# Winograd gate and up products of a decoder block: a sixth tile's first products beside the norms, down-weight sums in other tiles, one row tile transposed a turn sooner

## The chip, the core and the metric

One NeuronCore of a Trainium2 chip runs the whole kernel. TensorE (PE) multiplies, with its weight loads listed apart as PEld; VectorE (DVE), ScalarE (ACT) and GpSimd (POOL) do the elementwise work; SyncE (SP) issues the DMAs, which one queue takes in program order. The metric is the device time of one execution in microseconds (us); less is better.

## What is computed

One decoder layer in float32 on 1024 tokens of width 1024 with 16 meta tokens ahead of them. The part that the change touches is the end of the attention half and the SwiGLU half:

```python
h = h + rms_norm(mix @ w_out, ln_post_mix)
hn = rms_norm(h, ln_pre_ffn)
gu = hn @ w_gate_up                      # 1024 x 5632
ff = (silu(gu[..., :D_FF]) * gu[..., D_FF:]) @ w_down     # D_FF = 2816
h = h + rms_norm(ff, ln_post_ffn)
```

Each float32 product is made of three fp32r products: high by high, high by low and low by high part of operands that ACT (the rounded copy, a CAST) and DVE (the remainder, a subtraction) split.

## The kernel before

Gate and up are one Winograd scheme with seven half-size products in the place of eight. The hidden width is walked in `NF` = 22 tiles of 128 columns, `f_` = 0 to 21. A tile's seven products are of 12 matmuls each (four blocks of the inner dimension, three part products), and are numbered by `recipe`: 1 (`11` by `11`), 3 in the code of `first_products` or 2 in `recipe` (`12` by `21`), 5 (`s1` by `t1`), 6, 7, 3 and 4. The left operands `s1` to `s4` are sums of the weights that POOL makes (`combos`, tiles `cw`), the right operands `t1` to `t4` are sums of normed rows (`combine_rows`, tiles `c3`, `c1`, `c2`, `c4`), which PE then transposes.

**The norm stretch.** PE multiplies the last rows of the attention output (`half_out`, tiles `pz`), and beside that the row tiles `t` = 0 to 7 are normed in turns `n` = 0 to 9, written out by hand: ACT takes the sums of squares (`square_sum`, into `junk`; `ry` for the first norm, `rh` for the second), POOL the root, DVE `post_norm` and `second_norm`. `transposes` puts the two halves of a row tile through PE (tiles `tz` and `tzt`, from two PSUM banks, so that the third transposition waits until the remainder of the first is taken), ACT makes the high part (`b11h`, `b21h`, `bt3h` ...), DVE the low part (`b11l` ...). `unit()` emits the next piece of PE's other work in this stretch: 16 pieces of `half_out`, and then four pieces of six matmuls for each tile that is taken ahead: products 1 and 2 of tiles 3 and 4 (`SNAP`) and of 0, 1 and 2. The six PSUM banks hold those of tiles 0 to 2; those of 3 and 4 are copied to SBUF (`early`). `prepare_gate` loads a gate tile (`wgg`) and splits it into `a11` and `a12`, in the turns that `preps` names.

**The product stretch.** A loop over `f_` multiplies five products in tiles taken ahead (`ahead`) and seven in the others, all on PE in program order. Beside each product ACT and DVE split a block of the next tile, and POOL makes the sums of the next but one. Product 4 of an ahead tile is `held` until after the first product of the next. `store_acts` makes four sums of two finished tiles on POOL and stores them; `store_down` loads 256 rows of `w_down` (`rd`, one buffer of 1 MB), makes four sums on POOL and stores them (`down`). Both stand at the end of every second tile, from `f_` = 2 on. A last stretch multiplies the stored sums.

The engines keep the written order in both stretches; only SP's DMAs are ordered by the scheduler.

Of the kernel before, what the change touches and what calls it, by code (L numbers as in the profile page):

```python
# [21 lines left out]
P = 128  # L22
# [75 lines left out]
def hymba_kernel(ctx, tc, x, meta, rel_bias, g_pre_mix, g_post_mix, g_pre_ffn, g_post_ffn,  # L98
# [45 lines left out]
    dram = ctx.enter_context(tc.tile_pool(name="dram", bufs=1, space=DRAM))  # L144
# [1060 lines left out]
    def halves(t):  # L1205
        return y_of[t][:, 0:HALF], y_of[t][:, HALF:]

    def combine_rows(t):

        (b11, b21), (b12, b22) = halves(t - 4), halves(t)  # L1210
        t3, t1, t2, t4 = c = [bp.tile([P, HALF], F32, name=f"c{n}_{t}", tag="cb", bufs=6) for n in (3, 1, 2, 4)]
        rows_of[t] = dict(zip(("t3", "t1", "t2", "t4"), c))

        def first():
            pool.tensor_tensor(t3, b22, b12, op=ALU.subtract)
            pool.tensor_tensor(t1, b12, b11, op=ALU.subtract)

        return (first, lambda: pool.tensor_tensor(t2, t3, b11, op=ALU.add),
                lambda: dve.tensor_tensor(t4, b21, t2, op=ALU.subtract))

    rows_of = {}

# [8 lines left out]
        dve.tensor_tensor(lo, tp, f(hi), op=ALU.subtract)  # L1231


    op_homes = iter("gggg" + "wwww" + "gg" + "ggwww" + "oooow" + "ggggo" + "wwwwo" + "ggggo" + ("wwwwooo" + "ggggooo") * NF)
    o_n = [0]

    def op_tile(name):
# [69 lines left out]

    banks = {}

    N_AHEAD, SNAP = 5, (3, 4)  # L1310
    p1_of, early_of = {}, {}

    def first_products(f_):
        for i, (an, bn) in ((1, ("11", "11")), (3, ("12", "21"))):
            banks[f_, i] = b = bank(f"q{i}_{f_}")
            for part in range(2):
                product(b, f_, an, bn, True, i == 3, part)
                if part == 0:
                    yield None
            if f_ not in SNAP:  # L1320
                yield lambda: None
            elif i == 1:
                both = snp.tile([P, 2, HALF], F32, name=f"early{f_}")
                p1_of[f_], early_of[f_] = both[:, 0], both[:, 1]
                yield lambda f_=f_, b=b: act.copy(p1_of[f_], b)
            else:
                yield lambda f_=f_, b=b: dve.tensor_tensor(early_of[f_], b, p1_of[f_], op=ALU.add)

    def blocks():

# [20 lines left out]

    pinned.update(PINB)
    first_sum(2)
    preps = {0: 3, 1: 4, 4: 0, 5: 1, 6: 2}
    for n in range(4):
        gate = prepare_gate(preps[n], act) if n in preps else None
        if n:
            square_sum(n + 1, "rh", junk[0])
        unit(2)
        second_norm(n)  # L1360
        if n:
            transposes(halves(n - 1)[0], "11", n - 1)
        unit()
        if n:
            transposes(halves(n - 1)[1], "21", n - 1)
        unit()
        post_norm(n + 2)
        first_sum(n + 3)
        if gate:
            run(gate)  # L1370
    third = {}
    for n in range(4, 10):
        gate = prepare_gate(preps[n], act) if n in preps else None
        if n < 7:
            square_sum(n + 1, "rh", junk[0])
        if n == 6:
            b_op["t2"], b_op["t4"] = [[wap.tile([P, 4, HALF], F32R, name=f"bt{i}{x}", tag="wo", bufs=4) for x in "hl"]
                                      for i in (2, 4)]
            t1h, t1l, t3h = [h2p.tile([P, 4, HALF], F32R, name=f"b{x}", tag="late", bufs=3) for x in ("t1h", "t1l", "t3h")]
            b_op["t1"], b_op["t3"] = (t1h, t1l), (t3h, t3l)  # L1380
        if n >= 6:
            late = rows_of[n - 2]
            transposes(late["t3"], "t3", n - 2, third[n - 2])
        if n < NT:
            second_norm(n)
        if 5 <= n < 9:
            first, second, third[n - 1] = combine_rows(n - 1)
            first()
        if n == 4:
            transposes(halves(3)[0], "11", 3)  # L1390
        unit()
        if n >= 6:
            transposes(late["t1"], "t1", n - 2, (lambda: post_norm(n + 2)) if n + 2 < NT else lambda: None)
        elif n == 5:
            transposes(halves(4)[1], "22", 4, lambda: post_norm(7))
        else:
            post_norm(6)
        unit()
        if n == 4:
            transposes(halves(3)[1], "21", 3)  # L1400
        elif 6 <= n < 9:
            transposes(halves(n - 1)[1], "22", n - 1)
        first_sum(n + 3)
        if 5 <= n < 9:
            second()
        if n == 7:
            early = iter((raw_tile("cw00", (P, 2, 4, P)), bp.tile([P, 2, 4, P], F32, name="cw01", tag="gfb", bufs=1)))
            pending = combos(0, lambda name: next(early))
            pending[0]()
        elif n == 8:  # L1410
            pending[1]()
        unit()
        if n >= 6:
            transposes(late["t2"], "t2", n - 2)
        if n >= 7:
            unit()
        if n >= 6:
            transposes(late["t4"], "t4", n - 2)
        if gate:
            run(gate)  # L1420
    unit(20)
# [12 lines left out]
    def s_tile(f_, c):  # L1434
        s_of[f_, c] = fp.tile([P, HALF], F32, name=f"s{f_}{c}", tag="s", bufs=6)
        return s_of[f_, c]
# [63 lines left out]
        s4 = combined(f"s4_{i}", "S", ALU.subtract, a12, s2)  # L1500
        sp.dma_start(act_dram["4"][i], s4)

    def store_down(i):

        r = fp.tile([P, 2, 2, HALF], F32, name=f"rd{i}", tag="rd", bufs=1)
        sp.dma_start(r, w_down[0, 2 * i * P:2 * (i + 1) * P, :].rearrange("(j p) (h c) -> p j h c", p=P, h=2))
        (b11, b12), (b21, b22) = [[r[:, j, h] for h in range(2)] for j in range(2)]
        pool.tensor_tensor(b22, b22, b12, op=ALU.subtract)
        pool.tensor_tensor(b12, b12, b11, op=ALU.subtract)
        pool.tensor_tensor(b11, b22, b11, op=ALU.add)  # L1510
        pool.tensor_tensor(b21, b21, b11, op=ALU.subtract)
        for n, x in (("1", b12), ("2", b11), ("3", b22), ("4", b21)):
            sp.dma_start(down_dram[n][i], x)
# [29 lines left out]
            parts_of[n].append(hl)  # L1543

    held = None
    pending = combos(1, cw_tile)
    for f_ in range(NF):
        ahead = f_ < N_AHEAD
        order = (5, 6, 3, 7, 4) if ahead else (1, 5, 6, 2, 7, 3, 4)
        names = ("s1", "s2", "s4", "s3", "22") if f_ + 1 < N_AHEAD else ("11", "s1", "s2", "12", "s3", "s4", "22")  # L1550
        parts = [lambda: [load(n) for n in range(3)]] + [lambda: None] + [lambda n=n: split_step(n) for n in range(3)]
        if f_ + 1 < NF:
            first, second = pending
            parts = [lambda n=n: split_block(f_ + 1, n) for n in names]
            if len(order) < len(names):
                s2, s3 = parts[1:3], parts[3:5]
                parts = [parts[0], lambda: [c() for c in s2], lambda: [c() for c in s3]] + parts[5:]
            s0, s1 = parts[0:2]
            parts[0] = lambda: (first(), s0())
            parts[1] = lambda: (second(), s1())  # L1560
        parts = iter(parts)
        for i, n in enumerate(order):
            if n == 4 and ahead:
                held = f_
                next(parts, lambda: None)()
                continue
            if i == 0 and ahead:
                if f_ in SNAP:
                    s_of[f_, 0] = early_of[f_]
                    act.activation(early_of[f_], early_of[f_], AF.Silu)  # L1570
                else:
                    after(f_, 1)
                    after(f_, 2)
            multiply(f_, n, next(parts, lambda: None))
            if i == 0 and held is not None and held != f_:
                multiply(held, 4)
                held = None
        if f_ + 2 < NF:
            pending = combos(f_ + 2, cw_tile)
        j = f_ - 1  # L1580
        if j > 0 and j % 2:
            store_acts(j // 2)
            store_down(j // 2)
    store_down(NP - 1)
    store_acts(NP - 1)
    pinned.difference_update(("pe", "act", "dve", "pool"))
    op_st.close()
# [134 lines left out]
```

## Time and profile before

| | us |
|---|---|
| median of three runs | 1218.53 |
| lowest and highest | 1215.46, 1219.6 |
| the profiled execution | 1218.1 |
| its span, first to last instruction | 1216.1 |
| PE busy in the span | 1162.9 |
| DVE, ACT, POOL busy | 786.1, 551.4, 502.6 |

The span is what the trace covers; 2.0 us of the execution lie around it. Busy times are sums per engine. PE is busy in 96% of the span, so time can come only from stretches where it waits, where its clock is low, or from matmuls that leave a stretch in which it is full.

### The profile page before, as it was taken

Reading aid. Unit: us, or ns where it says so; the run is one execution under the profiler, and the core shown is the slowest. Engines: PE = TensorE matmul, PEld = TensorE weight load, DVE = VectorE, ACT = ScalarE, POOL = GpSimd, SP = SyncE. Lnnn points to the kernel's source line nnn. Section 1 sums busy time; section 2 is a strip of 40 time slices with the busy share of each in tenths; the row PEclk is TensorE's granted clock in tenths of the full one; section 3 lists DMA queues with packets and bytes.
Section 4 is the critical chain, followed back from the end, with each engine's and each line's share of the span. In section 5 each row is a group of like instructions: output and inputs, shape, how many; then the busy total and the mean of one; then the engine's idle time right before and its main releaser. Section 6 shows DMA issues by size and latency. Waiting matters only on the chain.

```text
span 1216.1 us, 17389 instructions
## 1 busy us (share of the span) xinstructions
PE 1162.9 (96%) x5967; PEld 987.1 (81%) x5967; DVE 786.1 (65%) x1637; ACT 551.4 (45%) x1174; POOL 502.6 (41%) x523
## 2 busy tenths in 40 slices
PE   7989999999999989987899999999999999999997
PEld 6978879998998777865787788888888887888886
DVE  6477876666666777888567755556555545556764
ACT  5366565555555451454442333333333325555531
POOL 7242334344333342326468665765566640000001
PEclk9999999999999999998999999999999999999999
DMA  7431223132121420363245545534455377676645
GB/s 231 133 97 30 57 66 101 45 80 59 41 69 41 148 87 26 97 241 104 79 138 189 175 164 185 175 134 157 147 183 173 129 252 260 224 236 214 225 151 196
DMA packets 135463, 168.36 MB, mean 138 GB/s; under 512 B 10644, under 2 KB 84372, under 8 KB 135374
## 3 DMA queue, kind: packets, MB, share of 16 engines
q1 hardware_dynamic: 135374, 167.25, 42.7%
q8 instruction: 47, 0.77, 0.3%
q14 instruction: 42, 0.34, 0.1%
HBM read 115.22 MB, written 46.56 MB: 133 GB/s over the span
## 4 chain that ended last, share of the span: by engine, by line
PE 43%; DVE 3%; POOL 3%; issue 2%; DMA 1%; ACT 1%; POOLq 0%; DVEq 0%; SPq 0%; ACTq 0%
PE q L113 26%; PE px L113 9%; PE py L113 7%; POOL rd L113 1%; POOL s L113 1%; DVE a L113 1%; DVE y L113 1%; DVE s L113 1%; POOL cw L113 0%; DMA rd<-in_w_down_dram 0%; PE tzt L113 0%; DVE as L113 0%; DMA act<-s 0%; DMA wgu<-in_w_gate_up_dram 0%; DMA rab<-in_w_down_dram 0%
## 5 line engine op out<-in xcount | busy, mean ns | idle before, releaser
L113 DVE TENSOR_TENSOR hl<-rab,hl 128x512 fp32r<-128x512 f32 x154 | 102.2, 712 | 76.8 <-ACT hl L113 76.5
L113 DVE TENSOR_TENSOR as<-cw,as 128x512 fp32r<-128x512 f32 x78 | 79.9, 1028 | 69.1 <-ACT as L113 68.1
L113 PE MATMUL px<-hl,hl 128*128 128x512 f32 x528 | 122.5, 393 | 1.7 <-ACT hl L113 1.5
L113 ACT CAST hl<-rab 128x512 fp32r<-128x512 f32 x154 | 88.1, 619 | 78.9 <-PE py L113 27.1
L113 PEld LDWEIGHTS px<-hl,hl 128*128 128x128 f32 x528 | 100.2, 190 | 23.4 <-ACT hl L113 1.9
L113 PE MATMUL py<-hl,hl 128*128 128x512 f32 x396 | 90.2, 389 | 0.0
L113 PEld LDWEIGHTS py<-hl,hl 128*128 128x128 f32 x396 | 74.3, 188 | 15.4
L113 ACT ACTIVATE s<-s 128x512 f32<-128x512 f32 x42 | 26.6, 632 | 111.5 <-DVE s L113 111.4
L113 POOL TENSOR_SCALAR PF<-PF,lf 128x144 f32<-128x144 f32 (+3 forms) x64 | 51.3, 801 | 62.4 <-DVE lf L113 46.0
L113 POOL TENSOR_TENSOR cw<-wgu 128x512 f32<-128x512 f32 x22 | 29.6, 1346 | 114.8 <-DMA wgu<-in_w_gate_up_dram 106.3
L113 POOL TENSOR_SCALAR rf0v<-sa 128x1 f32<-128x1 f32 x1 | 0.6, 563 | 177.2 <-DVE sa L113 177.2
L113 POOL TENSOR_TENSOR s<-s,s 128x512 f32<-128x512 f32 x41 | 60.7, 1493 | 30.0 <-DVE s L113 25.2
L113 POOL TENSOR_TENSOR rd<-rd 128x512 f32<-128x512 f32 x44 | 66.4, 1508 | 10.4 <-DMA rd<-in_w_down_dram 7.8
L113 ACT ACTIVATE PF<-PF,nf 128x144 f32<-128x144 f32 (+3 forms) x64 | 50.6, 790 | 39.2 <-DVE nf L113 37.7
L113 DVE TENSOR_TENSOR a<-wgg,a 128x512 fp32r<-128x512 f32 x44 | 48.1, 1101 | 30.1 <-ACT a L113 30.1
L113 PE MATMUL q<-b11h,a 128*128 128x512 f32 x176 | 60.8, 404 | 4.5 <-ACT b11h L113 4.5
L113 ACT CAST as<-cw 128x512 fp32r<-128x512 f32 x78 | 47.6, 619 | 33.9 <-POOL cw L113 22.6
L113 POOL TENSOR_SCALAR P<-P,ls 128x272 f32<-128x272 f32 (+1 forms) x64 | 29.5, 479 | 77.2 <-DVE ls L113 66.3
L113 DVE TENSOR_TENSOR s<-q,s 128x512 f32<-128x512 f32 x62 | 42.6, 687 | 27.3 <-PE q L113 26.3
L113 PE MATMUL q<-b21h,a 128*128 128x512 f32 x176 | 59.1, 394 | 0.7 <-ACT b21h L113 0.7
L113 ACT COPY s<-q 128x512 f32<-128x512 f32 x40 | 23.5, 587 | 79.7 <-PE q L113 57.5
L113 PE MATMUL q<-bt1h,as 128*128 128x512 f32 x176 | 58.0, 391 | 1.4 <-ACT as L113 1.2
(491 smaller groups left out, 3408.1 us busy)
## 6 DMA issues: line engine op xcount, KB each, us to landing
rab<-act SPq DMA_DIRECT2D x77, 256.0 KB, 3.1
act<-s SPq DMA_DIRECT2D x75, 256.0 KB, 2.7
wgg<-in_w_gate_up_dram SPq DMA_DIRECT2D x27, 512.0 KB, 4.2
wgu<-in_w_gate_up_dram SPq DMA_DIRECT2D x22, 512.0 KB, 3.6
rd<-in_w_down_dram SPq DMA_DIRECT2D x11, 1024.0 KB, 6.9
down<-rd SPq DMA_DIRECT2D x44, 256.0 KB, 2.0
rab<-down SPq DMA_DIRECT2D x44, 256.0 KB, 3.3
wi<-in_w_in_dram SPq DMA_DIRECT2D x18, 512.0 KB, 3.7
```

Source lines behind the costliest of these rows:

```text
L113: i = fn(*a, **k)
```

## The change

It has three parts. First, `N_AHEAD` is 6 and `SNAP` has a third tile: tile 5's products 1 and 2 are made in the norm stretch, after those of 3 and 4. `prepare_gate` is called once more (tile 5 in turn 4, tiles 0, 1 and 2 one turn later each), and there are four more calls of `unit()`. The copies of tile 5 go to DRAM (`keep`, two stores) and come back at the start of `f_` = 4 (`bring_back`, two loads). Room for them is had by making `t2` and `t4` in place, in the row tiles themselves: `combine_rows` takes two new tiles of four buffers and not four of six. Second, row tile 3 is transposed at the end of turn 3, not within turn 4. Third, `store_down` is parted: `load_down` issues the load at the start of a tile and the sums stand at its end, in odd tiles from 5 on and in 12 and 18. The table of buffers (`op_homes`) is written anew to fit.

```diff
-        t3, t1, t2, t4 = c = [bp.tile([P, HALF], F32, name=f"c{n}_{t}", tag="cb", bufs=6) for n in (3, 1, 2, 4)]
-        rows_of[t] = dict(zip(("t3", "t1", "t2", "t4"), c))
+        t3, t1 = [bp.tile([P, HALF], F32, name=f"c{n}_{t}", tag="cb", bufs=4) for n in (3, 1)]
+        rows_of[t] = {"t3": t3, "t1": t1, "t2": b11, "t4": b21}
...
-        return (first, lambda: pool.tensor_tensor(t2, t3, b11, op=ALU.add),
-                lambda: dve.tensor_tensor(t4, b21, t2, op=ALU.subtract))
+        return (first, lambda: pool.tensor_tensor(b11, t3, b11, op=ALU.add),
+                lambda: dve.tensor_tensor(b21, b21, b11, op=ALU.subtract))
...
-    N_AHEAD, SNAP = 5, (3, 4)
+    N_AHEAD, SNAP = 6, (3, 4, 5)
     p1_of, early_of = {}, {}
+
+    snap_dram = dram.tile([P, 2, HALF], F32, name="snap_dram")
+
+    def keep(f_, b):
+        dve.tensor_tensor(early_of[f_], b, p1_of[f_], op=ALU.add)
+        if f_ == 5:
+            for i, x in enumerate((p1_of[f_], early_of[f_])):
+                sp.dma_start(snap_dram[:, i], x)
+
+    def bring_back(f_):
+        early_of[f_] = s_tile(f_, 0)
+        p1_of[f_] = fp.tile([P, HALF], F32, name=f"p1_{f_}", tag="s", bufs=6)
+        for i, x in enumerate((p1_of[f_], early_of[f_])):
+            sp.dma_start(x, snap_dram[:, i])
...
-    preps = {0: 3, 1: 4, 4: 0, 5: 1, 6: 2}
+    preps = {0: 3, 1: 4, 4: 5, 5: 0, 6: 1, 7: 2}
...
+        if n == 3:
+            transposes(halves(3)[0], "11", 3)
+            transposes(halves(3)[1], "21", 3)
         post_norm(n + 2)
...
-        if n == 4:
-            transposes(halves(3)[0], "11", 3)
         unit()
...
-        if n == 4:
-            transposes(halves(3)[1], "21", 3)
-        elif 6 <= n < 9:
+        if 6 <= n < 9:
...
-        if n >= 7:
+        if n >= 6:
             unit()
-        if n >= 6:
             transposes(late["t4"], "t4", n - 2)
+        if 7 <= n < 9:
+            unit()
...
+        if f_ == 4:
+            bring_back(5)
+
+        rd = load_down(n_down) if f_ >= 5 and (f_ % 2 or f_ in (12, 18)) else None
...
         if j > 0 and j % 2:
             store_acts(j // 2)
-            store_down(j // 2)
-    store_down(NP - 1)
+        if rd is not None:
+            store_down(n_down, rd)
+            n_down += 1
```

What stands where is shown at three places. The first is ACT at turns 3 and 4 (`b11h` from `tz112` is row tile 2, from `tz113` row tile 3; `sry6` and `srh5` are sums of squares of row tiles 6 and 5). Before:

```order
L113 CAST b11h_6542<-tz112_6765 128x4x128
L113 CAST b21h_6544<-tz212_6780 128x4x128
L113 ACTIVATE junk_6376,sry6_6796<-y6_5343 128x1024
L113 ACTIVATE junk_6376,srh5_6804<-y5_5342 128x1024
L113 CAST b11h_6542<-tz113_6811 128x4x128
L113 CAST b21h_6544<-tz213_6836 128x4x128
L113 ACTIVATE junk_6376,sry7_6843<-y7_5344 128x1024
L113 COPY early3_6835<-q1_3_6818 128x512
```

and now:

```order
L113 CAST b11h_6542<-tz112_6766 128x4x128
L113 CAST b21h_6544<-tz212_6781 128x4x128
L113 CAST b11h_6542<-tz113_6794 128x4x128
L113 CAST b21h_6544<-tz213_6801 128x4x128
L113 ACTIVATE junk_6376,sry6_6811<-y6_5343 128x1024
L113 ACTIVATE junk_6376,srh5_6819<-y5_5342 128x1024
L113 ACTIVATE junk_6376,sry7_6844<-y7_5344 128x1024
L113 COPY early3_6843<-q1_3_6826 128x512
```

Both casts of row tile 3 moved ahead of the squares of row tiles 6, 5 and 7.

The second is PE in turns 6 and 7 (`tzt24` is `t2` of row tile 4, `tzt44` its `t4`, `tzt35` `t3` of row tile 5; `q1_5` is product 1 of tile 5; the rows of matmuls up to the next transposition are one unit of six). Before:

```order
L113 MATMUL tzt24_6983<-ident_70,c2_4_6874 128x128 x4
L113 MATMUL tzt44_6990<-ident_70,c4_4_6875 128x128 x4
L113 MATMUL tzt35_7003<-ident_70,c3_5_6940 128x128 x4
L113 MATMUL q1_0_6975<-b11h_6542,a11_0_6857 128x512
L113 MATMUL q1_0_6975<-b11l_6543,a11_0_6857 128x512
L113 MATMUL q1_0_6975<-b11h_6542,a11_0_6857 128x512 x2
L113 MATMUL q1_0_6975<-b11l_6543,a11_0_6857 128x512
L113 MATMUL q1_0_6975<-b11h_6542,a11_0_6857 128x512
L113 MATMUL tzt15_7024<-ident_70,c1_5_6941 128x128 x4
```

and now:

```order
L113 MATMUL tzt24_6980<-ident_70,y0_5337 128x128 x4
L113 MATMUL q1_5_6972<-b11h_6542,a11_5_6858 128x512
L113 MATMUL q1_5_6972<-b11l_6543,a11_5_6858 128x512
L113 MATMUL q1_5_6972<-b11h_6542,a11_5_6858 128x512 x2
L113 MATMUL q1_5_6972<-b11l_6543,a11_5_6858 128x512
L113 MATMUL q1_5_6972<-b11h_6542,a11_5_6858 128x512
L113 MATMUL tzt44_6994<-ident_70,y0_5337 128x128 x4
L113 MATMUL tzt35_7009<-ident_70,c3_5_6939 128x128 x4
L113 MATMUL q3_5_7022<-b21h_6544,a12_5_6861 128x512
```

A unit stands between the transpositions of `t2` and `t4` where there was none, and the units here are tile 5's in the place of tile 0's.

The third is POOL at tiles 2 to 5 of the product stretch (`s1_0` to `s4_0` are the sums of `store_acts` for tiles 0 and 1, `rd0` the first down sums, `cw40` and `cw41` the weight sums of tile 4). Before:

```order
L113 TENSOR_TENSOR s1_0_7514<-s01_7265,s11_7363 128x512
L113 TENSOR_TENSOR s2_0_7517<-s1_0_7514,s00_7229 128x512
L113 TENSOR_TENSOR s01_7265<-s00_7229,s01_7265 128x512
L113 TENSOR_TENSOR s4_0_7522<-s10_7313,s2_0_7517 128x512
L113 TENSOR_TENSOR rd0_7525<-rd0_7525 128x512 x4
L113 TENSOR_TENSOR cw40_7509<-wgu4_7507 128x512
L113 TENSOR_TENSOR cw40_7509<-cw40_7509,wgg4_7505 128x512
L113 TENSOR_TENSOR cw41_7510<-wgg4_7505,wgu4_7507 128x512
L113 TENSOR_TENSOR cw41_7510<-wgg4_7505,cw40_7509 128x512
```

and now:

```order
L113 TENSOR_TENSOR s4_0_7554<-s10_7345,s2_0_7549 128x512
L113 TENSOR_TENSOR cw40_7541<-wgu4_7539 128x512
L113 TENSOR_TENSOR cw40_7541<-cw40_7541,wgg4_7537 128x512
L113 TENSOR_TENSOR cw41_7542<-wgg4_7537,wgu4_7539 128x512
L113 TENSOR_TENSOR cw41_7542<-wgg4_7537,cw40_7541 128x512
L113 TENSOR_TENSOR cw50_7652<-wgu5_7650 128x512
L113 TENSOR_TENSOR cw50_7652<-cw50_7652,wgg5_7648 128x512
L113 TENSOR_TENSOR cw51_7653<-wgg5_7648,wgu5_7650 128x512
L113 TENSOR_TENSOR cw51_7653<-wgg5_7648,cw50_7652 128x512
L113 TENSOR_TENSOR s1_1_7758<-s21_7494,s31_7605 128x512
```

The four down sums that stood ahead of tile 4's weight sums are gone from here; the first now stand behind those of tile 6. SP's rows at the end of that tile show what is queued behind the second load of down weights (`wgu7` is the up tile for `f_` = 7). Now:

```order
L113 DMA down1_0_156<-rd0_7769 128x512
L113 DMA down2_0_167<-rd0_7769 128x512
L113 DMA down3_0_178<-rd0_7769 128x512
L113 DMA down4_0_189<-rd0_7769 128x512
L113 DMA act11_2_81<-early4_6908 128x512
L113 DMA rd1_8042<-in_w_down_dram 128x2x1024
L113 DMA wgu7_7871<-in_w_gate_up_dram 128x8x128
L113 DMA wgg8_8022<-in_w_gate_up_dram 128x8x128
```

`rd1` is issued behind the four stores of `rd0`, whose buffer it takes, and `wgu7` behind `rd1`; before, at the same tile's load, `wgu7` stood behind `rd2` and one store of activations.

## Rows read from the trace of the kernel before

**Rows 1.** Stretches by window: length, busy time (count) per engine, PEclk, DMA share, GB/s.

```profile
540.00:550.00 10.00, 3.86 (x20) 2.59 (x18) 9.93 (x11) 4.19 (x8) 2.85 (x4) 0.78 0.16 66
550.00:560.00 10.00, 8.45 (x25) 6.08 (x26) 5.09 (x8) 3.90 (x10) 1.47 (x4) 0.71 0.23 94
...
750.00:800.00 50.00, 50.00 (x222) 41.42 (x221) 27.08 (x31) 17.94 (x32) 28.40 (x19) 1.00 0.48 155
```

**Rows 2.** Timeline of PE, norm stretch: start, length, what, count [idle before, releaser].

```profile
545.26 0.84 PE L113 MATMUL tz<-ident,y 128*128 128x128 f32 x4 [2.24 <-DVE b11l L113]
550.64 0.80 PE L113 MATMUL q<-b11h,a 128*128 128x512 f32 x1 [4.54 <-ACT b11h L113]
...
565.49 0.66 PE L113 MATMUL tzt<-ident,c 128*128 128x128 f32 x4 [1.42 <-POOL c L113]
```

**Rows 3.** Timeline of ACT at turns 4 and 5.

```profile
548.97 1.06 ACT L113 ACTIVATE junk<-y 128x1024 f32<-128x1024 f32 x1 [2.95 <-DVE y L113]
...
556.69 0.59 ACT L113 CAST b21h<-tz 128x512 fp32r<-128x512 f32 x1 [6.10 <-PE tz L113]
...
559.73 1.07 ACT L113 ACTIVATE junk<-y 128x1024 f32<-128x1024 f32 x1
```

**Rows 4.** Timeline of DVE at turns 3 to 5.

```profile
545.72 0.68 DVE L113 TENSOR_TENSOR b21l<-tz,b21h 128x512 fp32r<-128x512 f32 x1
...
550.62 0.69 DVE L113 TENSOR_TENSOR b11l<-tz,b11h 128x512 fp32r<-128x512 f32 x1 [0.57 <-ACT b11h L113]
...
557.31 0.69 DVE L113 TENSOR_TENSOR b21l<-tz,b21h 128x512 fp32r<-128x512 f32 x1 [2.95 <-ACT b21h L113]
559.35 1.30 DVE L113 TENSOR_TENSOR a<-wgg,a 128x512 fp32r<-128x512 f32 x2 [1.35 <-ACT a L113]
```

**Rows 5.** Waits of PE from 530 to 970 us: in total, times, longest.

```profile
PE tz L113 <- DVE bt3l L113: 2.3, 2, 1.5
...
PE tzt L113 <- DVE bt1l L113: 1.0, 2, 0.8
PE tzt L113 <- DVE bt2l L113: 1.0, 1, 1.0
```

**Rows 6.** Timeline of PE, first matmul of the product stretch.

```profile
600.07 0.53 PE L113 MATMUL q<-bt1h,as 128*128 128x512 f32 x1 [1.24 <-ACT as L113]
```

**Rows 7.** Timeline of PE, tiles 3 to 5 of the product stretch.

```profile
651.11 0.47 PE L113 MATMUL q<-bt3h,as 128*128 128x512 f32 x1 [1.28 <-DVE s L113]
...
667.53 0.39 PE L113 MATMUL q<-b11h,a 128*128 128x512 f32 x1
...
671.61 0.50 PE L113 MATMUL q<-bt4h,a 128*128 128x512 f32 x1 [1.20 <-DVE p L113]
```

**Rows 8.** Timeline of POOL, the same tiles.

```profile
638.99 6.50 POOL L113 TENSOR_TENSOR rd<-rd 128x512 f32<-128x512 f32 x4
645.45 1.29 POOL L113 TENSOR_TENSOR cw<-wgu 128x512 f32<-128x512 f32 x1
...
668.67 6.81 POOL L113 TENSOR_TENSOR rd<-rd 128x512 f32<-128x512 f32 x4
678.38 1.29 POOL L113 TENSOR_TENSOR cw<-wgu 128x512 f32<-128x512 f32 x1 [2.90 <-DMA wgu<-in_w_gate_up_dram]
```

**Rows 9.** Timeline of DVE, the same tiles.

```profile
669.17 1.78 DVE L113 TENSOR_TENSOR mix<-cw,mix 128x512 fp32r<-128x512 f32 x1
670.88 0.68 DVE L113 TENSOR_TENSOR p<-q,p 128x512 f32<-128x512 f32 x1
...
688.01 0.68 DVE L113 TENSOR_TENSOR mix<-cw,mix 128x512 fp32r<-128x512 f32 x1
```

**Rows 10.** DMA issues on the page: count, KB each, us to landing.

```profile
wgu<-in_w_gate_up_dram SPq DMA_DIRECT2D x22, 512.0 KB, 3.6
rd<-in_w_down_dram SPq DMA_DIRECT2D x11, 1024.0 KB, 6.9
down<-rd SPq DMA_DIRECT2D x44, 256.0 KB, 2.0
```

More of the change, by code (lines that the diff above doesn't have):

```diff
@@ L1231, in transposes @@
         dve.tensor_tensor(lo, tp, f(hi), op=ALU.subtract)
-    op_homes = iter("gggg" + "wwww" + "gg" + "ggwww" + "oooow" + "ggggo" + "wwwwo" + "ggggo" + ("wwwwooo" + "ggggooo") * NF)
+    op_homes = iter("gggg" + "wwww" + "gggg" + "wwwwg" + "oooog" + "wwwwo" + "ggggo" + "wwwwo" + "ggggo" + ("wwwwooo" + "ggggooo") * NF)
     o_n = [0]
@@ L1322, in first_products @@
             elif i == 1:
-                both = snp.tile([P, 2, HALF], F32, name=f"early{f_}")
+                both = (snp if f_ < 5 else bp).tile([P, 2, HALF], F32, name=f"early{f_}")
                 p1_of[f_], early_of[f_] = both[:, 0], both[:, 1]
@@ L1326, in first_products @@
             else:
-                yield lambda f_=f_, b=b: dve.tensor_tensor(early_of[f_], b, p1_of[f_], op=ALU.add)
+                yield lambda f_=f_, b=b: keep(f_, b)
     def blocks():
@@ L1501, in store_acts, with load_down, store_down @@
         sp.dma_start(act_dram["4"][i], s4)
-    def store_down(i):
+    def load_down(i):
         r = fp.tile([P, 2, 2, HALF], F32, name=f"rd{i}", tag="rd", bufs=1)
         sp.dma_start(r, w_down[0, 2 * i * P:2 * (i + 1) * P, :].rearrange("(j p) (h c) -> p j h c", p=P, h=2))
+        return r
+    def store_down(i, r):
         (b11, b12), (b21, b22) = [[r[:, j, h] for h in range(2)] for j in range(2)]
@@ L1545, in hymba_kernel @@
     held = None
+    n_down = 0
     pending = combos(1, cw_tile)
@@ L1582, in hymba_kernel @@
             store_acts(j // 2)
-            store_down(j // 2)
-    store_down(NP - 1)
+        if rd is not None:
+            store_down(n_down, rd)
+            n_down += 1
+    assert n_down == NP
     store_acts(NP - 1)
```

## The prediction, written before the changed kernel ran

> **What bounds the kernel now.** I read the windows by stage first. In the product stretch PE is full: 222 matmuls fill 50.00 of 50 us at the full clock, 0.225 us each, and DVE, ACT and POOL have idle time [rows 1]. A matmul that leaves this stretch is worth its whole 0.225 us. In the norm stretch it is otherwise: from 540 to 550 us DVE is busy for 9.93 of 10 us and PE for 3.86, and PE's granted clock is 0.78 there and 0.71 in the next 10 us, which is the 1.2 GHz level for part of both [rows 1]. So this stretch is bound by the chain from row tile to row tile, and PE has room. The timeline of PE names its two large waits: 2.24 us for `b11l`, and 4.54 us for `b11h` of row tile 3 [rows 2]. The timelines of ACT and DVE tell why. The cast of `b11h` stood behind the square of row tile 5, which waited 2.95 us for DVE's `post_norm`; the cast of `b21h` came 6.10 us later, since its transposition stands behind the first unit of products on PE; and the square of row tile 6, behind it, starts only at 559.73 [rows 3]. DVE meanwhile lost 0.57, 2.95 and 1.35 us [rows 4], 4.87 in all, though it was the engine that bounds.
>
> **Part 1, row tile 3 a turn sooner.** Nothing is added; eight transposing matmuls, two casts and two remainders change places. The first transposition can go no sooner than 545.26, since it still waits for the bank that row tile 2's `b11l` gives back [rows 2]. The second follows when `b21l` of row tile 2 ends, 545.72 + 0.68 = 546.40 [rows 4]. Each then goes through ACT (0.59 us a cast [rows 3]) and DVE. I count 0.3 us of DVE idle for each of the two, 0.6 in all, for the 4.87 that vanish, since `post_norm` of row tile 5, 6 and 7 and `second_norm` now follow one another without a cast between. DVE is thus 4.3 us ahead at the remainder of `b22`. ACT's square of row tile 6 no longer stands behind the late `b21h`; it now waits for `post_norm` of row tile 6 and starts about 4.3 us sooner, and with it the root on POOL and POOL's first `t3`, for which PE waited until 565.49 [rows 2]. That becomes 561.2. What is late next is still POOL's `t3`, at the same place. PE's first products of tile 3 can start at about 547.4, at the low clock, but they end before 561.2 at either level, so their speed costs nothing.
>
> **Part 2, tile 5 taken ahead.** Out of the product stretch go products 1 and 2 of tile 5: 24 matmuls x 0.225 = 5.4 us [rows 1]. The same 5.4 us enter the norm stretch after 561.2. Before, from 565.49 to the first product of tile 0 at 600.07 it was 34.6 us [rows 2, 6]. In these lie waits of 2.3, 1.0 and 1.0 us for `bt3l`, `bt1l` and `bt2l` [rows 5], 4.3 together, and at the end 1.24 us for the first weight split [rows 6], which stays. How much of 5.4 do the waits take up? The unit between `t2` and `t4` in turn 6 covers the 1.0 for `bt2l` and part of one for `bt1l`; those for `bt3l` stay in the main, since `bt3l` stands on DVE behind the two gate splits of each turn. The other three units stand in turns 7 and 8, where part of the waits remains. On the other side POOL now halts in turn 7: the first weight sums of tile 0 go into a raw buffer that the gate tile of turn 7 holds until DVE has split it. This stops no one before turn 9, and without POOL beside it DVE is faster: a remainder with both inputs in SBUF took 1.78 us while POOL worked and 0.68 alone, and a sum that reads PSUM took 0.68 even beside POOL [rows 8, 9]. I take 1.3 us as hidden. So the products start at 561.2 + 34.6 + 5.4 - 1.3 = 599.9, 0.2 us sooner than before. The bounds: with all of 5.4 hidden it is 4.3 sooner, the shift of part 1 alone (the waits sum to just 4.3, so this is a floor); with none hidden 561.2 + 34.6 + 5.4 = 601.2, 1.1 later.
>
> The Trainium skill ("GPSIMD Engine Reference", Key points) states that GpSimd shares its SBUF interfaces with VectorE and contends with its instructions of two SBUF inputs. The rows agree, with 1.78 against 0.68. If the page's rule were applied to every remainder of turns 7 and 8 as gained time, the start would come near the floor of the range above.
>
> What else comes with tile 5: one more copy on ACT, one more sum on DVE, and two casts and two remainders that leave tile 4's share of the product stretch for turn 7, where DVE and ACT have gaps. The four transfers of 256 KB (two stores, two loads) stand on SP behind nothing that waits long, and the loads have a whole tile's time; I cost them at nothing. If a load were late, PE would wait at the start of `f_` = 5; the load of twice that size takes 3.6 us [rows 10]. Reading tile 5's copies gives DVE a few more sums of 0.68 us, as tiles 3 and 4 have now. The in-place `t2` and `t4` are as many instructions as before.
>
> **Part 3, down sums elsewhere.** At `f_` = 2 POOL made four down sums, 6.50 us from 638.99, and the weight sums of tile 4 started only behind them, at 645.45 [rows 8]; ACT and DVE got their splits late, and PE waited 1.28 us at 651.11 [rows 7]. Now no down sum stands there, so tile 4's weight sums start 6.5 us sooner and this wait goes. At the end of `f_` = 4 PE waited 1.20 us for DVE's `p`, at 671.61 [rows 7], which stood behind a remainder of 1.78 us beside the down sums of 668.67 [rows 8, 9]. The down sums of the new first place come at the end of `f_` = 5, which is now the last tile taken ahead and the one with seven blocks to split in five products, so the same crowding moves there; but POOL starts them as soon as tile 6's weight sums are done, since the load is long there, and may be through when `p` comes. The trace can't decide between 0 and 1.2; I take half, 0.6. Beyond that PE shows no wait until the down stretch, so the load's 6.9 us [rows 10] that POOL no longer waits for are worth nothing there.
>
> **The sum**, against the profiled execution of 1218.1: 5.4 out of the product stretch, 0.2 by its earlier start, 1.28 and 0.6 of waits, 7.5 us in all: 1210.6. The median of the runs lies 0.4 above the profiled one, so 1211.0. By the bounds it is best 5.4 + 4.3 + 1.28 + 1.2 = 12.2 us, 1206.3, and at worst 5.4 - 1.1 = 4.3 us, 1214.2, if the waits of part 3 only move.
>
> **Rivals.** *Low clock again.* In the norm stretch the clock fell while PE waited and came back in the dense matmuls behind [rows 1, 2]. Now PE is done with tile 3 and the first half of tile 4 some 2 or 3 us before 561.2 and waits again. If the clock falls there, some 5 us of matmuls run at half speed, 2.5 us, of which little is hidden: 1213.5. Against it: the wait is about as long as the 2.24 that stands first in [rows 2], and part of it falls right behind 24 dense matmuls. The Trainium skill ("TensorE: Matmul & The Clock Gate", Part 1) has the array fall to its lower level when it idles; the trace agrees, and by that rule this rival is the one to expect if the wait grows.
>
> *The stretch grows, the waits move.* DVE or the banks bind in turns 6 to 8 with nothing hidden, tile 5 as a copied tile costs DVE at `f_` = 5 what tile 4 did, and both waits of part 3 come back one tile on, with 1 to 2 us for the extra sums of DVE. For it speaks how crowded DVE was there, with 1.78 us for one remainder right before `p` [rows 9]. It is 5.4 - 1.1 - 2 = 2.3 us: 1216.2, no change that can be told.
>
> *Slower: the up tile behind the down load.* `rd1` waits on SP until the stores of `rd0` have landed, and `wgu` of the tile after next stands behind it. If it comes late, POOL's weight sums are late, ACT is held at their cast with the copies behind it that free PSUM, and PE waits in product 7; the same in each of eight tiles with such a load. The price is what POOL starts later than some 10 us into the tile: at `f_` = 5 it started at 678.38, 10.85 after 667.53 [rows 7, 8], with no wait of PE from it, in a tile longer than the common one. By the rows, four weight sums of 1.29 us or more and four down sums of 6.5 to 6.8 [rows 8] end some 13 us into a tile, the stores take 2.0, then `rd` 6.9 and `wgu` 3.6 one after the other [rows 10], so `wgu` is there 6.5 us into the next tile of 84 x 0.225 = 18.9 us, 3 us before it decides. If the loads slowed each other by 5 us more, it would be 1.5 us in eight tiles: 1211 + 12 = 1223.
>
> That the change does nothing is out: PE's order shows tile 5's units in the norm stretch.
>
> **How the numbers follow.** The forecast has 0.60, the low clock 0.13, the grown stretch 0.19, the late up tile 0.08. The range leaves out the last and the outer edges of the others: 1206.5 to 1216.5. About 0.3%, 3.7 us, is what a measurement of this kernel can tell from no change, so faster means under 1214.9: the forecast, the low clock but for a little, and 0.05 of the grown stretch, 0.76 in all; the rest of the latter two is no change, 0.17; slower 0.07.
>
> **What would show it.** In the profile after: ACT's casts of `b11h` and `b21h` one behind the other at about 546 and 547; the first `tzt` at about 561; the first product of tile 0 near 600, so that the whole gain of 7 lies behind it; no wait of PE in `f_` = 3, and one of 0 to 1.2 us at the end of `f_` = 5. A first `tzt` at 565 would break part 1; a product stretch that starts after 602, part 2; a wait of PE in each odd tile from 7 on would be the slower rival.

## The result, and where the time went

The changed kernel takes 1237.78 us (median of four runs, 1235.58 to 1241.5) against 1216.99 before: 1.0167 times, 95% interval 1.0134 to 1.0199. That is slower by 20.8 us where 7.5 less was forecast.

The three stages tell where. The norm stretch is counted from the transposition that waits 2.2 us for `b11l` of row tile 2 to the first product of tile 0, the product stretch from there to the end of PE's last product (the first `px` less its wait), the down stretch from there to the end:

| us, from one trace each | norm stretch | product stretch | down stretch |
|---|---|---|---|
| before [rows 2, 6] | 54.81 | 395.62 | 220.4 |
| after | 55.04 | 420.57 | 219.6 |

The stages add up to 24.4 us more. In this trace the norm stretch also began 4.5 us sooner than before, at 540.76 where it was 545.26, so that the whole span is 19.9 us longer; the last section comes back to that.

The norm stretch came out close to what the prediction had. The timeline of PE after; the rows answer to [rows 2, 6]:

```profile
540.76 0.66 PE L113 MATMUL tz<-ident,y 128*128 128x128 f32 x4 [2.23 <-DVE b11l L113]
...
557.15 1.12 PE L113 MATMUL tzt<-ident,c 128*128 128x128 f32 x4 [4.47 <-POOL c L113]
...
595.80 0.50 PE L113 MATMUL q<-bt1h,as 128*128 128x512 f32 x1 [1.19 <-ACT as L113]
```

ACT casts row tile 3 in one go now, where [rows 3] had 6.10 us and the square between:

```profile
541.45 0.58 ACT L113 CAST b11h<-tz 128x512 fp32r<-128x512 f32 x1 [0.99 <-PE tz L113]
543.11 0.59 ACT L113 CAST b21h<-tz 128x512 fp32r<-128x512 f32 x1 [1.07 <-PE tz L113]
```

From 540.76 the first `tzt` is 16.39 us away, before it was 20.23; the first product is 55.04 us away, before 54.81. The loss lies behind it, in the product stretch. Its windows (columns as in [rows 1]):

```profile
700.00:800.00 100.00, 96.53 (x422) 78.69 (x421) 53.39 (x60) 33.32 (x59) 61.48 (x40) 1.00 0.42 141
800.00:900.00 100.00, 90.59 (x377) 73.36 (x376) 48.95 (x51) 30.66 (x55) 58.48 (x39) 0.95 0.51 171
900.00:1000.00 100.00, 92.03 (x385) 74.20 (x386) 55.70 (x58) 30.17 (x54) 67.65 (x45) 0.97 0.46 157
```

Where [rows 1] had 222 matmuls in 50 us, 444 in 100, there are now 422, 377 and 385, and the granted clock is under 1.00 in two of three windows. The waits of PE from 600 to 1000 us (in total, times, longest):

```profile
PE q L113 <- ACT s L113: 17.9, 9, 3.0
PE q L113 <- DVE p L113: 3.5, 5, 0.7
```

That is 21.4 us. One of these waits, in tile 8, is followed back here through four engines. PE comes first (the first row is the start of tile 8), then ACT:

```profile
717.20 0.39 PE L113 MATMUL q<-b11h,a 128*128 128x512 f32 x1
...
729.13 0.50 PE L113 MATMUL q<-bt3h,as 128*128 128x512 f32 x1 [0.89 <-ACT s L113]
```

```profile
726.60 0.62 ACT L113 CAST as<-cw 128x512 fp32r<-128x512 f32 x1 [5.54 <-POOL cw L113]
...
727.97 0.62 ACT L113 CAST as<-cw 128x512 fp32r<-128x512 f32 x1 [0.27 <-POOL cw L113]
728.50 0.58 ACT L113 COPY s<-q 128x512 f32<-128x512 f32 x1
```

Product 7 adds to what product 6 left in its PSUM bank, and the copy `s<-q` must have read that bank before. That copy stands on ACT behind the casts of tile 9's `s1` and `s2`, and ACT was held 5.54 us for them. POOL, with the time that it waited before each:

```profile
708.11 6.57 POOL L113 TENSOR_TENSOR rd<-rd 128x512 f32<-128x512 f32 x4
725.27 1.29 POOL L113 TENSOR_TENSOR cw<-wgu 128x512 f32<-128x512 f32 x1 [10.59 <-DMA wgu<-in_w_gate_up_dram]
...
731.28 6.48 POOL L113 TENSOR_TENSOR s<-s,s 128x512 f32<-128x512 f32 x4
742.36 1.29 POOL L113 TENSOR_TENSOR cw<-wgu 128x512 f32<-128x512 f32 x1 [4.60 <-DMA wgu<-in_w_gate_up_dram]
...
765.78 1.29 POOL L113 TENSOR_TENSOR cw<-wgu 128x512 f32<-128x512 f32 x1 [10.82 <-DMA wgu<-in_w_gate_up_dram]
```

And SP's queue (start and length of the issues):

```profile
709.87 5.16 SPq L113 DMA_DIRECT2D down<-rd  x4
...
715.60 1.86 SPq L113 DMA_DIRECT2D act<-s  x1
718.62 0.38 SPq L113 DMA_DIRECT2D rd<-in_w_down_dram  x1
719.09 0.42 SPq L113 DMA_DIRECT2D wgu<-in_w_gate_up_dram  x1
...
720.19 17.92 SPq L113 DMA_DIRECT2D act<-s  x6
738.20 0.39 SPq L113 DMA_DIRECT2D wgu<-in_w_gate_up_dram  x1
```

POOL, SP and the transfers close a loop. POOL ends the down sums at 708.11 + 6.57 = 714.68. SP, which stood at their stores, issues the last of them and must then wait until they have landed before `rd` may go into the same buffer (718.62); from 700 to 780 us the profile puts two waits of SP, 1.9 us, down to `down<-rd`. Only then comes `wgu` (719.09). At 725.27, 6.18 us after that issue and 10.59 us after its last work, POOL can go on. The other up tile stands behind six stores of the activations' sums, the last of which waits for POOL too: 4.60 us more. Before, in tiles of the same kind, POOL waited for `wgu` like this:

```profile
862.74 1.29 POOL L113 TENSOR_TENSOR cw<-wgu 128x512 f32<-128x512 f32 x1 [4.59 <-DMA wgu<-in_w_gate_up_dram]
...
876.58 1.29 POOL L113 TENSOR_TENSOR cw<-wgu 128x512 f32<-128x512 f32 x1 [7.46 <-DMA wgu<-in_w_gate_up_dram]
```

That is 12.05 us in a pair of tiles, and the next pair began at 900.80, 38.06 us behind the first: POOL kept PE's pace. In the changed kernel two tiles cost POOL 765.78 - 725.27 = 40.5 us, of which 4.60 + 10.82 = 15.4 are waits for its own tail. PE needs 2 x 84 x 0.225 = 37.8 us for two tiles. So POOL falls back 2.7 us in each pair of tiles; once the lead that it had is used up, PE waits about that long.

### The profile page after: what moved, and what is told of

The parts are those of the page before. It is cut to its first block, busy times and chain, and to the rows that moved or that the text cites. A ratio compares the mean times of both kernels' runs of the same rounds, so it can differ in the third digit from the quotient of the medians.

```text
span 1236.0 us, 17396 instructions
## 1 busy us (share of the span) xinstructions
PE 1166.4 (94%) x5967; PEld 985.4 (80%) x5967; DVE 786.4 (64%) x1640; ACT 550.7 (45%) x1172; POOL 508.7 (41%) x523
## 4 chain that ended last, share of the span: by engine, by line
PE 55%; POOL 14%; DMA 11%; DVE 9%; issue 8%; ACT 3%; SPq 0%; POOLq 0%; DVEq 0%; ACTq 0%
PE q L113 11%; PE px L113 9%; PE py L113 7%; DMA wgu<-in_w_gate_up_dram 6%; POOL cw L113 5%; POOL rd L113 3%; PE pvb L113 3%; POOL s L113 3%; PE pqb L113 3%; PE of L113 3%; PE pqa L113 2%; PE pk L113 2%; PE sf L113 2%; PE tf L113 2%; PE pya L113 1%
## 5 line engine op out<-in xcount | busy, mean ns | idle before, releaser
L113 DVE TENSOR_TENSOR as<-cw,as 128x512 fp32r<-128x512 f32 x79 | 91.7, 1165 | 119.0 <-ACT as L113 116.8
L113 DVE TENSOR_TENSOR hl<-rab,hl 128x512 fp32r<-128x512 f32 x154 | 99.5, 691 | 78.2 <-ACT hl L113 77.6
L113 PEld LDWEIGHTS py<-hl,hl 128*128 128x128 f32 x396 | 74.4, 188 | 15.4
L113 POOL TENSOR_TENSOR s<-s,s 128x512 f32<-128x512 f32 x41 | 63.8, 1573 | 20.5 <-DVE s L113 18.3
L113 PE MATMUL q<-bt3h,as 128*128 128x512 f32 x136 | 50.0, 431 | 15.0 <-ACT s L113 15.0
L113 PE MATMUL q<-bt2h,as 128*128 128x512 f32 x176 | 57.8, 389 | 0.0
```

Source lines behind the costliest of these rows:

```text
L113: i = fn(*a, **k)
```

## Experiments

Theory A was that part 3 alone makes the loss, by this loop. The rivals were tile 5's way through DRAM, the mere number of sums and stores, and the sharing of the DMA engines.

| | median, us | to before | 95% interval | norm stretch | product stretch |
|---|---|---|---|---|---|
| before | 1215.66, 1216.15 | 1 | | 54.81 | 395.62 |
| parts 1 and 2 | 1211.01 | 0.996 | 0.9939 to 0.9981 | 55.05 | 394.21 |
| part 3 alone | 1245.93 | 1.0246 | 1.0198 to 1.0294 | 54.78 | 421.38 |
| load of `rd` on ACT's queue | 1207.92 | 0.9935 | 0.9911 to 0.9959 | 55.04 | 387.41 |
| down sums at even tiles | 1211.57 | 0.9963 | 0.9943 to 0.9984 | 55.05 | 391.58 |
| SP as written | 1210.51 | 0.9956 | 0.9937 to 0.9975 | 55.05 | 388.00 |
| half the down load | 1226.86 | 1.0090 | 1.0067 to 1.0113 | 55.06 | 404.14 |
| part 3 on ACT's queue | 1214.19 | 0.9980 | 0.9964 to 0.9996 | 54.95 | 392.62 |
| part 1 alone | 1211.71 | 0.9963 | 0.9950 to 0.9976 | 50.98 | 397.09 |

The four kernels from parts 1 and 2 to down sums at even tiles are compared with the runs of before that have the first median, the last four with those that have the second.

**Parts 1 and 2.** In the changed kernel, part 3 undone:

```diff
-        rd = load_down(n_down) if f_ >= 5 and (f_ % 2 or f_ in (12, 18)) else None
...
             store_acts(j // 2)
-        if rd is not None:
-            store_down(n_down, rd)
...
+            store_down(j // 2, load_down(j // 2))
+    store_down(NP - 1, load_down(NP - 1))
...
```

> The changed kernel with its part 3 undone: the down weights are loaded and summed where the kernel before has it. Theory A (the loss is made by part 3 alone, in a loop of POOL, the stores and the up tile's load): the 24 matmuls of tile 5 leave the product stretch and nothing waits in its regular tiles, so it is 5 to 6 us less than the kernel before, about 1211.5 where that has 1217, with PE waits of about 1.3 and 1.2 us in tiles 3 to 5 back. Rival B (the loss comes with tile 5: its copies' way through DRAM, or the in-place t2 and t4): still over 1230, with waits of PE for ACT in the regular tiles.

It gave 1211.01, and no wait within the products of a regular tile (one that is not taken ahead). Tile 5 and its copies are not the cause. But the early tiles cost more than [rows 7] had:

```profile
650.21 0.47 PE L113 MATMUL q<-bt3h,as 128*128 128x512 f32 x1 [1.93 <-DVE s L113]
...
686.28 0.50 PE L113 MATMUL q<-bt4h,mix 128*128 128x512 f32 x1 [3.14 <-DVE p L113]
```

1.93 and 3.14 us where there were 1.28 and 1.20: with tile 5 ahead the crowding that part 3 was to undo is worse, so of tile 5's 5.4 us only 395.62 - 394.21 = 1.4 are left in the product stretch. Behind the second wait the granted clock was 0.64 for 4.7 us.

**Part 3 alone**, the same edit in the kernel before.

> The kernel before with part 3 alone: loads at the start and sums at the end of odd tiles from 5 on and of 12 and 18. Theory A: the waits of the changed kernel in product 7 of the regular tiles come here too, 1 to 3 us in eight or nine tiles, and the clock falls behind the longest; the changed kernel lost 20.8 us although tile 5 should have given 5 to 6, so this loses 24 to 28: 1241 to 1245 where before has 1217. Rival B: within 2 us of before.

1245.93, slower by 30: more than expected. Its waits of PE from 595 to 1030 us have the same line on top,

```profile
PE q L113 <- ACT s L113: 15.8, 8, 3.1
```

and its product stretch is 25.8 us longer than before (3.7 of the rest lie ahead of the norm stretch, see the last section). Part 3 is the cause: without it there is no loss, and alone it is enough.

**The load on ACT's queue.** One word in the changed kernel:

```diff
-        sp.dma_start(r, w_down[0, 2 * i * P:2 * (i + 1) * P, :].rearrange("(j p) (h c) -> p j h c", p=P, h=2))
+        act.dma_start(r, w_down[0, 2 * i * P:2 * (i + 1) * P, :].rearrange("(j p) (h c) -> p j h c", p=P, h=2))
```

> The changed kernel, but the load of the down weights is issued by ACT at the start of its tile and not by SP, so the up tile's load no longer stands behind it. Theory A1 (of the loop, the place of that load ahead of the up tile's is what breaks it): POOL's loop falls from 40.5 us for two tiles to about 6 + 6.5 + 4.6 + 6 + 6.5 + 4.6 = 34, under PE's 37.8, the waits in the regular tiles go, and it is 6 to 8 us less than before, about 1210. Rival A2 (two sets of sums and stores ahead of two up tiles are enough, with the load or without): waits stay at over 1 us in each second tile, 1225 or more.

1207.92: 30 us less than the changed kernel, 7.7 less than before. POOL, in the same tiles:

```profile
699.52 1.29 POOL L113 TENSOR_TENSOR cw<-wgu 128x512 f32<-128x512 f32 x1 [4.58 <-DMA wgu<-in_w_gate_up_dram]
...
705.42 6.19 POOL L113 TENSOR_TENSOR rd<-rd 128x512 f32<-128x512 f32 x4
716.19 1.29 POOL L113 TENSOR_TENSOR cw<-wgu 128x512 f32<-128x512 f32 x1 [4.58 <-DMA wgu<-in_w_gate_up_dram]
...
733.59 1.29 POOL L113 TENSOR_TENSOR cw<-wgu 128x512 f32<-128x512 f32 x1 [4.67 <-DMA wgu<-in_w_gate_up_dram]
```

The wait behind the down sums fell from 10.59 to 4.58 us and the loop from 40.5 to 34.1, under PE's 37.8; PE is busy in 383.76 of 384 us:

```profile
600.00:984.00 384.00, 383.76 (x1692) 317.11 (x1690) 233.60 (x258) 136.57 (x244) 253.30 (x168) 1.00 0.53 175
```

The two sets of sums and stores do no harm by themselves, so rival A2 falls. The Trainium skill ("DMA: Bandwidth & Descriptors", Rules for kernel authors) says that spreading DMAs over issuing engines brings no bandwidth and saves only issue time. No bandwidth was wanted here; what was saved is the time that a queue stood at a load that could not go yet, with an urgent one behind it.

**Down sums at even tiles.** Parts 1 and 2, sums at tiles 5 and 13, then in every second tile from 6 on behind the activations' sums:

```diff
-        rd = load_down(n_down) if f_ >= 5 and (f_ % 2 or f_ in (12, 18)) else None
...
-        if rd is not None:
-            store_down(n_down, rd)
+        if f_ > 5 and f_ % 2 == 0 or f_ in (5, 13):
+            store_down(n_down, load_down(n_down))
             n_down += 1
...
+    store_down(NP - 1, load_down(NP - 1))
...
```

> Parts 1 and 2, with no down sums at tiles 2 and 4: they stand at tiles 5 and 13 and, as in the kernel before, right behind the activations' sums of every second tile from 6 on, one set behind the last tile. Theory A: from 6 on one hold of the up tile by POOL for two tiles, no loop; the waits of 1.3 and 1.2 us in tiles 3 to 5 are gone, so it is 2 us less than parts 1 and 2 alone, about 1209.5. Rival C: each single odd place (5 and 13) brings a wait of 1 to 3 us in the tiles behind it, and nothing is won against parts 1 and 2 alone.

1211.57, no gain over parts 1 and 2 in the median, though its product stretch is 2.6 us shorter. Rival C was half right: the place at tile 5 costs a wait of 0.51 us, and the other odd place, 13, brings one wait of 2.87 us in tile 15, since POOL has tile 14's two sets of sums to make right behind it (the row is shown below, with the clock). The places with one hold for two tiles bring none.

**SP as written.** The changed kernel with SP in the written order too:

```diff
+    pinned.add("sp")
     for f_ in range(NF):
...
```

> The changed kernel, with SP too kept in the written order in the product stretch. The load of the down weights then stands at the start of its tile, ahead of that tile's sums and a whole tile behind the stores of the last ones, so it no longer waits for stores just made; the up tile still stands right behind it on SP. Theory A1 in its closer form (the loss needs the load to stand between fresh down stores and an up tile that POOL wants at once): no wait of PE in the regular tiles, 1207 to 1209 as with the load on ACT's queue. Rival D (an up tile that shares the DMA engines with the load is late anyway): waits of about 1 us in every second tile, 1215 to 1222.

1210.51, a little over the expected 1207 to 1209; the product stretch of 388.00 us is that of the load on ACT's queue within 0.6, and no regular tile waits within its own products. SP, then POOL:

```profile
701.93 0.43 SPq L113 DMA_DIRECT2D rd<-in_w_down_dram  x1
...
711.57 0.37 SPq L113 DMA_DIRECT2D wgu<-in_w_gate_up_dram  x1
712.04 2.34 SPq L113 DMA_DIRECT2D down<-rd  x4
```

```profile
707.85 6.19 POOL L113 TENSOR_TENSOR rd<-rd 128x512 f32<-128x512 f32 x4
716.03 1.29 POOL L113 TENSOR_TENSOR cw<-wgu 128x512 f32<-128x512 f32 x1 [2.00 <-DMA wgu<-in_w_gate_up_dram]
```

Now `rd` goes ahead of the sums of its own tile and `wgu` ahead of their stores. The load was written at the start of its tile; the scheduler had put it a tile earlier, right behind the stores that it must wait for.

Rival D, an up tile that is late because it shares the DMA engines with the load, was not put to the test by this: here `wgu` is issued 711.57 - 701.93 = 9.64 us behind `rd`. The trace of the load on ACT's queue has a case of both at once: SP issued `wgu` at 695.38, ACT the load at 696.60, and POOL used `wgu` at 699.52, 4.14 us after its issue, as long as with no load beside it. An up tile ahead of the load was not late there; the late ones stand behind it.

**Half the down load.** The load is 128 rows and leaves out the second block of rows; the sums are as many, two of them made from the first block instead:

```diff
-        sp.dma_start(r, w_down[0, 2 * i * P:2 * (i + 1) * P, :].rearrange("(j p) (h c) -> p j h c", p=P, h=2))
+        sp.dma_start(r[:, 0], w_down[0, 2 * i * P:(2 * i + 1) * P, :].rearrange("p (h c) -> p h c", h=2))
...
```

> The changed kernel with half of each load of down weights: 128 rows, 512 KB; the second row block is left out and the four sums are made from the first, with as many instructions. The up tile behind it landed 6.2 us after its issue in the changed kernel and 3.7 us with the load on ACT's queue. If the transfer is what makes it late, half of the 2.5 us goes, POOL's loop is 39.2 us against 40.5, and of the excess over PE's 37.8 about half is left: some 10 us of waits and fewer falls of the clock, 1216 to 1224. If the wait of the load for the landing of the stores is it, nothing changes: 1234 to 1238. If the loop has little margin the other way, all goes: 1208.

1226.86, above the window by 3, with about half of the loss left. POOL:

```profile
703.48 1.29 POOL L113 TENSOR_TENSOR cw<-wgu 128x512 f32<-128x512 f32 x1 [4.57 <-DMA wgu<-in_w_gate_up_dram]
...
709.51 6.08 POOL L113 TENSOR_TENSOR rd<-rd 128x512 f32<-128x512 f32 x4
725.55 1.28 POOL L113 TENSOR_TENSOR cw<-wgu 128x512 f32<-128x512 f32 x1 [9.97 <-DMA wgu<-in_w_gate_up_dram]
...
742.53 1.29 POOL L113 TENSOR_TENSOR cw<-wgu 128x512 f32<-128x512 f32 x1 [4.43 <-DMA wgu<-in_w_gate_up_dram]
```

The loop is 742.53 - 703.48 = 39.05 us where 39.2 was expected; the excess over 37.8 is 1.25 in the place of 2.7, and the product stretch is 16.7 us over the 387.41 of the load on ACT's queue, against 33.2 in the changed kernel. The loss goes with the loop's excess. How POOL's wait divides is seen on SP, first in the kernel with the load on ACT's queue, then in this one:

```profile
712.05 0.39 SPq L113 DMA_DIRECT2D wgu<-in_w_gate_up_dram  x1
```

```profile
718.42 0.46 SPq L113 DMA_DIRECT2D wgu<-in_w_gate_up_dram  x1
```

From the end of the down sums to the issue of `wgu` it is 712.05 - 711.61 = 0.44 us with no load in front, 718.42 - 715.59 = 2.83 here and 719.09 - 714.68 = 4.41 in the changed kernel; from the issue to POOL it is 4.14 (the expectation had 3.7), 7.13 and 6.18. So both count, the hold of SP until the stores have landed and the transfer in front. Which of the two the missing half takes its 1.4 us from is not resolved: the landing of `wgu` is no shorter here.

**Part 3 on ACT's queue**: the kernel before with part 3 and `act.dma_start` for its load.

> The kernel before with part 3, its load issued by ACT: what part 3 is worth without its loop. The waits of 1.28 us in tile 3 and 1.20 at tiles 4 and 5 go: 2.0 to 2.5 us less than before, about 1213. Rival: the sums' new places bring a wait of their own, no difference from before. With tile 5 ahead the same edit is worth more by the runs so far: 1211.0 with the old places, 1207.9 with the new.

1214.19: 2.0 us less, the small end of what was expected. Part 3 without its loop is worth 3.0 us of the product stretch, and with tile 5 ahead 394.21 - 387.41 = 6.8.

**Part 1 alone**: the two calls of `transposes` for row tile 3 moved to the end of turn 3.

> The kernel before with row tile 3 transposed at the end of turn 3, and nothing else. The norm stretch from the transposition that waits for b11l of row tile 2 to the first product of tile 0 was 54.81 us before and 55.04 with parts 1 and 2. By the prediction's working part 1 takes 4.3 us off it: 50.7 us, and the whole 3.5 to 4.3 us under before, about 1211.7. Rival: what part 1 gains is taken up by waits for bt3l and the others in turns 5 to 8, 52.5 us or more, and the whole within 2 us of before; then tile 5's units cost less than their 5.4 us because part 1 left them room.

1211.71, as expected, and the norm stretch 50.98 us, 3.8 shorter; the product stretch is 1.5 us longer, with 2.34 us of waiting in tile 3 where there were 1.28. The timeline of PE:

```profile
547.96 1.05 PE L113 MATMUL tz<-ident,y 128*128 128x128 f32 x4 [2.23 <-DVE b11l L113]
...
564.36 1.12 PE L113 MATMUL tzt<-ident,c 128*128 128x128 f32 x4 [4.73 <-POOL c L113]
```

The first `tzt` is 16.40 us behind it, as in the changed kernel.

## Why the prediction was wrong

**Part 1: right.** Forecast 4.3 us off the way to the first `tzt`, measured 3.84; alone it takes 3.83 off the stretch. POOL's `t3` is late next, at the same place, as said (4.47 us in the changed kernel).

**Part 2 in the norm stretch: right.** Of tile 5's 5.4 us, 1.3 were to be hidden; 55.04 - 50.98 = 4.06 were added, so 1.34 were. What hides them was not told apart; the working has the four new pieces of tile 5 in turns 6, 7 and 8, but by the loops of the two kernels `unit()` is called three times more, not four, and the fourth piece falls to turn 9. In the product stretch parts 1 and 2 take off 392.62 - 387.41 = 5.2 us (both with part 3's load on ACT's queue), forecast 5.4.

**The low clock: its condition came true, its price did not.** PE waited 4.47 us, longer than the rival supposed, and the clock fell:

```profile
557.15:562.15 5.00, 5.00 (x16) 4.20 (x17) 5.00 (x6) 1.59 (x4) 4.75 (x5) 0.52 0.61 194
```

That is 5 us of matmuls at about half speed, as the rival said, but DVE is busy for all 5.00 of them too, and it bounds there. The price shows between before and part 1 alone, from the first `tzt` on, where the clock was at the upper level in one and fell in the other:

```profile
565.50:570.50 5.00, 4.18 (x23) 3.26 (x24) 5.00 (x5) 1.73 (x4) 4.83 (x5) 1.00 0.59 189
```

```profile
564.40:569.40 5.00, 5.00 (x18) 4.19 (x19) 5.00 (x5) 1.68 (x4) 4.83 (x5) 0.58 0.60 191
```

From the first `tzt` to the first product it is 600.07 - 565.49 = 34.58 us before and 598.94 - 564.36 = 34.58 with part 1 alone: the low clock cost nothing there, where the rival had 2.5 us.

**Part 3's gain: right in kind, forecast too small.** Forecast 1.28 + 0.6; alone 3.0 in the product stretch, and beside tile 5 6.8, since there parts 1 and 2 alone wait 1.93 and 3.14 us.

**The sum without the loop** was 7.5 us; the two kernels that have all three parts and no loop gained 7.74 and 5.64 (SP as written). That the first is so close is in part luck: tile 5 and part 3 are not separate terms, as the 3.0 and 6.8 above show.

**The step that failed** is the price of the rival called slower, the up tile behind the down load. Its mechanism and its place (product 7, through ACT's copies) are what happened; it was put at 0.08 because of the sentence that `wgu` "is there 6.5 us into the next tile", "3 us before it decides". Four things were wrong in it.

- The point from which it decides is not 10 us. It was read from one tile, at `f_` = 5 in the kernel before, whose blocks are split in another order. From tile 8's rows: product 7 could have begun at 729.13 - 0.89 = 728.24, and from POOL's start at 725.27 to 729.13 it is 3.86, so POOL had to start by 724.38, which is 7.2 us after the tile's first product at 717.20.
- The arrival was 725.27 - 717.20 = 8.07 us into the tile, not 6.5. The working let POOL begin the tile with its weight sums; in fact it began them 3.9 us into tile 7, because that tile's `wgu` is held as well, behind the stores of the activations' sums. I costed one hold of SP by POOL and there are two in a pair. The transfers, put at 2.0 + 6.9 + 3.6 = 12.5 us one after the other, took 10.59, which hid part of this error. PE's first row of tile 7, and POOL's:

```profile
698.16 0.39 PE L113 MATMUL q<-b11h,a 128*128 128x512 f32 x1
```

```profile
702.09 1.29 POOL L113 TENSOR_TENSOR cw<-wgu 128x512 f32<-128x512 f32 x1 [4.63 <-DMA wgu<-in_w_gate_up_dram]
```

- A wait of 1.5 us in eight tiles supposes that each tile begins anew. The loop has no such start: what counts is its length against PE's, 40.5 to 37.8. I added up one way through the loop, but not the loop. The prediction's own figures would have given it, as an estimate: 13 us of sums and 12.5 of transfers for the tile with the down sums, as many sums, 13, and 3.6 for the up tile in the other, 42.1 us.
- In this rival the clock was not priced. Of the 33.2 us by which the product stretch exceeds that of the load on ACT's queue, 21.2 are waits (21.4 less the 0.2 that is there too) and 12.0 are not. By the windows of 700 to 1000 us above, about 8 of these are the low clock: 0.05 x 100 = 5 us in the second and 0.03 x 100 = 3 in the third. The other 4 are neither, and were not told apart.

The test that the prediction named, a wait in each odd tile from 7 on, was close: the waits come in the even tiles from 8 to 20, and in 13 and 19 as well, behind the extra sets of sums in 12 and 18.

## What to carry to other kernels

When a load is moved, write out the closed loop through the queue: which compute ends it, which stores and landings stand between, which load behind it the same compute wants next; its length for one period goes against the bound engine's period, and the lead only delays the loss. A prefetch into a single buffer waits for the last user's stores to land, and on an ordered queue everything behind it waits too (here `wgu` went out 4.41 us behind the sums, and 0.44 with nothing in front): give it a queue with nothing urgent, or place it a full period behind those stores. Check where a scheduler really puts it; "at the start of the tile" in the code was a tile earlier on the queue.

## What was unexpected of the hardware

**The clock after a wait.** Windows of PE behind some of the waits (PEclk, the granted clock, is the third number from the right), first in the changed kernel, last in the one with the down sums at even tiles:

```profile
859.00:864.00 5.00, 4.97 (x15) 3.99 (x16) 3.79 (x4) 1.95 (x4) 4.92 (x4) 0.67 0.05 20
...
987.20:992.00 4.80, 4.80 (x14) 3.82 (x15) 3.60 (x4) 1.91 (x4) 4.72 (x4) 0.65 0.01 5
```

```profile
866.50:872.00 5.50, 5.45 (x24) 4.43 (x24) 4.29 (x5) 2.18 (x4) 2.23 (x2) 1.00 0.60 191
```

The waits ahead of them:

```profile
859.03 0.79 PE L113 MATMUL q<-bt3h,as 128*128 128x512 f32 x1 [3.00 <-ACT s L113]
...
987.19 0.50 PE L113 MATMUL q<-bt3h,as 128*128 128x512 f32 x1 [1.94 <-ACT s L113]
```

```profile
866.55 0.50 PE L113 MATMUL q<-bt3h,mix 128*128 128x512 f32 x1 [2.87 <-ACT s L113]
```

The clock went to the 1.2 GHz level for part of the next 5 us behind 3.00 and behind 1.94 us of waiting, and stayed at 2.4 GHz behind 2.87. In the changed kernel it fell at five waits, of 2.61, 2.82, 3.00, 2.95 and 1.94 us (before 811.67, 835.15, 859.03, 964.29 and 987.19), and behind its waits of 0.89 to 1.61 us for ACT's copies it did not. A fall cost about 1.6 us: 15 matmuls in the 5 us behind 859.00, where 22 fit at 0.225. That is some 8 us for the five, on top of 13.3 us of waits that led to them. The Trainium skill ("TensorE: Matmul & The Clock Gate", Part 1) has the array slow down when it idles; the rows agree that it does, but the length of the wait did not tell here whether it would. What does tell was not tried.

**The first half.** The orders of the engines up to 530 us are the same in all these kernels, yet the norm stretch began between 540.76 and 548.96 us. In the six kernels with part 2 it was 540.76 to 543.65, in the four without 545.26 to 548.96. The medians don't follow that throughout: the load on ACT's queue gained 7.74 us where its two stretches alone give 8.21 - 0.23 = 7.98, but parts 1 and 2 gained 4.65 where theirs give 1.41 - 0.24 = 1.17, and the changed kernel lost 20.8 where they give 25.2. One trace of each kernel doesn't settle it, and the cause stays open. The norm stretch, by contrast, came out within 0.02 us in six kernels (55.04 to 55.06). The down stretch, whose products no part of the change touches, did not: it was 218.5 us with parts 1 and 2 and 220.4 before. So a change of some microseconds is better read from its stages than from one span, but what the stages give and what the medians give can lie some microseconds apart here.
